# A feed-forward block with Strassen's seven products: block sums written in place, two of eight K pairs, a bank of its own for the shared product

## The chip, the cores and the metric

The kernel runs on one core of one Trainium2 chip. The time is device microseconds from start to end of one execution; it is measured several times and the median is given. Five engines work in parallel, each on its own queue of instructions in a fixed order: TensorE (PE, with its weight loads shown apart as PEld), VectorE (DVE), ScalarE (ACT), GpSimd (POOL) and SyncE (SP), which issues the transfers from memory. They wait for one another by semaphores.

## The reference

Two layers on 256 tokens of width 2048: layer 0 is a Mamba-2 mixer, layer 1 differential attention; each is followed by a SwiGLU feed-forward block of width 5632, with RMS norms around every part. Everything is float32. The change touches the two feed-forward blocks alone:

```python
def swiglu(h, w_gate, w_up, w_down):
    return (jax.nn.silu(h @ w_gate) * (h @ w_up)) @ w_down

for i in range(DEPTH):                      # DEPTH = 2
    x = x + rmsnorm(mixer(rmsnorm(x)))      # SSD in layer 0, attention in layer 1
    h = rmsnorm(x, norm_ffn_pre[i])
    x = x + rmsnorm(swiglu(h, ffn_w_gate[i], ffn_w_up[i], ffn_w_down[i]), norm_ffn_post[i])
```

Here h is 256 x 2048, the gate and up weights 2048 x 5632, the down weights 5632 x 2048.

## The kernel before

**Split numbers.** Every product of float32 numbers is made of three matmuls. A helper, `prep`, splits a piece of weights: ACT rounds it to `hi` (line 118), and DVE makes `lo` = raw minus `hi` (line 119). With the activations split likewise (`xT_hi`, `xT_lo`) a product is hi times hi, hi times lo and lo times hi, added up in one PSUM bank. A matmul takes 128 x 128 activations as its stationary side and 128 x 512 weights as its moving side.

**Where weights lie.** `rawp` has three buffers of 128 x 2048 float32 (1 MB), into which SP loads weights. `hlB` has four buffers for `hi` and four for `lo`. `accp` and `auxp` are four PSUM banks each: all eight that there are. `t512` tiles (eight buffers) hold results.

**The stage in question.** An `ffn` goes through the 5632 columns in chunks of 512. Chunk 10 runs through the plain routine `mv`; chunks 0 to 9 run two at a time through `pair` (line 200), once with the gate weights and once with the up weights: five couples of a gate call and an up call in a block, so twenty calls of `pair` in the kernel. A call computes four results of 128 x 512, named (t, c) for token half t and column half c, over eight K pairs (`kp` 0 to 7). A K pair is 256 rows of weights by 1024 columns, one `raw` buffer, loaded by two transfers of 512 KB (line 230).

- A plain K pair does the 2 x 2 by 2 x 2 block product as eight products, which is 24 matmuls, six for each (t, c). It needs one `prep`.
- A K pair of the first `NSTR` = 3 does it with Strassen's seven products (Winograd's form): 21 matmuls. For these DVE adds up four sums of weight blocks into a second tile, `sums`, which takes another of the three `rawp` buffers (lines 245 to 247); `prep` is run on three blocks of the raw weights and on the four sums, so two of the `hlB` buffers are used. Sums of activations (`form`) are made once in a block by `make_forms`. Products p1, p5 and p6 are added up in banks of `auxp`; the product that two results share is added up in the bank of (1, 1), from which DVE reads it after the third K pair, while later products still have to be added there. Then DVE makes the combinations s1, w and u (lines 262 to 265).

After the last K pair `done` adds the combination to each (t, c): for the gate into a fresh tile `g`, with Silu by ACT (lines 748, 749), for the up call into `y`, followed by the product with `g` (lines 758, 759). After an up call each `g` is turned by four transposes on PE and split again (`act_piece`, line 276), and after two, four and four chunks `out_proj` multiplies with the down weights through `mv`.

**What sets the order.** The program is written in straight lines; a scheduler gives each engine a fixed order of its own at build time and takes pool buffers as they come free. An engine whose next instruction has to wait does not go on to another.

Of the kernel before, what the change touches and what calls it, by code (L numbers as in the profile page):

```python
# [10 lines left out]
F32 = mybir.dt.float32  # L11
# [20 lines left out]
NSTR = 3  # L32
# [3 lines left out]
def trunk_kernel(ctx, tc, x_rows, x_cols, vec_cols, vec64, post_rows, lam_rows,  # L36
# [163 lines left out]
    def pair(blocks, ns, form, done):  # L200

        flush()
        acc = {}
        begun = set()

        def bank(k):
            if k not in acc:
                acc[k] = (auxp if k in ("p1", "p5", "p6") else accp).tile(
                    [P, 512], F32, tag="aux" if k in ("p1", "p5", "p6") else "acc", name=f"c{k}"
                    if isinstance(k, str) else "acc")
            return acc[k]

        def mm(k, st, hi, lo, last):
            ps = bank(k)

            again = k == (1, 1) and ns > 0
            for q, (a, b) in enumerate(((st[0], hi), (st[0], lo), (st[1], hi))):
                nc.tensor.matmul(ps, a, b, start=k not in begun, stop=last and q == 2, skip_group_check=again)  # L223
                begun.add(k)

        ss = {}
        for kp, src in enumerate(blocks):
            raw = rawp.tile([P, 4, 512], F32, tag="raw", name="raw")
            for c in range(2):
                nc.sync.dma_start(raw[:, 2 * c:2 * c + 2], src[c])  # L230
            if kp >= ns:
                hi, lo = prep(raw)
                for t in range(NT):
                    for c, slots in ((0, (2, 3)), (1, (0, 1))):
                        for j in range(2):
# [12 lines left out]
            hi, lo = prep(raw[:, 1:4])
            sh, sl = prep(sm)
            k0, k1 = 2 * kp, 2 * kp + 1  # L250
            mm("p1", x_stat(k0, 0), hi[:, 1], lo[:, 1], last)
            mm((0, 0), x_stat(k1, 0), hi[:, 2], lo[:, 2], last and ns == len(blocks))
            mm("p5", form(kp, 0), sh[:, 1], sl[:, 1], last)
            tick()
            mm((0, 1), form(kp, 3), hi[:, 0], lo[:, 0], last and ns == len(blocks))
            mm("p6", form(kp, 2), sh[:, 2], sl[:, 2], last)
            mm((1, 0), x_stat(k1, 1), sh[:, 3], sl[:, 3], last and ns == len(blocks))
            mm((1, 1), form(kp, 1), sh[:, 0], sl[:, 0], last)
            tick()
            if last:  # L260
                s1, w, u = (t512(n) for n in ("s1", "sw", "su"))
                nc.scalar.copy(s1, acc["p1"])
# [3 lines left out]
                ss.update({(0, 0): (s1, ALU.add), (0, 1): (w, ALU.add), (1, 0): (u, ALU.subtract), (1, 1): (w, ALU.add)})  # L266
# [440 lines left out]
    def ffn(wg, wu, wd, step, final):  # L707
# [36 lines left out]
        def g_done(p):  # L744
            def done(t, c, ps, ss):
                g = gt[(t, 2 * p + 1 - c)] = t512("g")
                s, op = ss[(t, c)]
                nc.vector.tensor_tensor(g, ps, s, op=op)
                nc.scalar.activation(g, g, AF.Silu, scale=rs(t))
            return done  # L750

        def u_done(p):
            def done(t, c, ps, ss):
                ch = 2 * p + 1 - c
                g = gt[(t, ch)]
                s, op = ss[(t, c)]
# [217 lines left out]
```

## Time and profile before

| | us |
|---|---|
| median of 3 runs | 2629.34 (2629.06 to 2629.64) |
| the profiled execution's own time | 2630.26 |
| its span, first to last instruction | 2628.5 |
| PE busy | 2566.6 (98%), 12210 matmuls |
| weight loads busy | 2099.3 (80%) |
| DVE busy | 1873.6 (71%) |
| ACT busy | 1308.1 (50%) |

A busy PE in this table is not PE at its peak: a matmul of 512 columns is shown with some 390 ns, while in a full pipeline one starts every 227 ns. So a matmul that starts late is seen in the spacing of the starts, that is, in how long a stretch with a known number of matmuls takes, and less in PE's idle time. The rows that follow later give such stretches.

### The profile page before, as it was taken

To read this page: it belongs to the slowest core of one execution; us is meant where nothing else is said; L and a number is where in the kernel's file an instruction comes from. 1 tells how busy PE (TensorE), PEld (TensorE's weight loads), DVE (VectorE), ACT (ScalarE), POOL (GpSimd) and SP (SyncE) were. 2 spreads that over 40 slices of the span, in tenths; PEclk is the share of its full clock that TensorE was granted. 3 is DMA by queue.
4 is the path that set the end of the run, shared out by engine and by line. 5 is a ranking of instruction groups with operands and counts; after the bars stand their busy time and mean duration, and the time that the engine had idled before them with its cause. 6 is when DMAs were issued, how large, how long until landed. Compare 5 with 4: busy or idle time off the path is not lost.

```text
span 2628.5 us, 31177 instructions
## 1 busy us (share of the span) xinstructions
PE 2566.6 (98%) x12210; PEld 2099.3 (80%) x12210; DVE 1873.6 (71%) x2250; ACT 1308.1 (50%) x1526; POOL 158.5 (6%) x164
## 2 busy tenths in 40 slices
PE   8999999999999999999999999999999999999998
PEld 7878888887877877788788788887787777887776
DVE  7888758886787577757775666556686588667864
ACT  4555555555565345435453544445654445434542
POOL 2021000120100000000001100001100000000001
PEclk9999999999999999999999999999999999999999
DMA  6545555454746445554665544544546455645463
GB/s 220 192 145 193 190 194 178 175 177 163 276 165 234 166 160 209 208 176 163 214 232 206 193 147 161 176 156 143 214 177 208 162 190 186 216 163 205 169 249 138
DMA packets 111699, 492.10 MB, mean 187 GB/s; under 512 B 10880, under 2 KB 27584, under 8 KB 75712
## 3 DMA queue, kind: packets, MB, share of 16 engines
q1 hardware_dynamic: 110896, 489.27, 53.2%
q8 instruction: 96, 1.57, 0.2%
q10 hardware_dynamic: 656, 0.85, 0.1%
q14 instruction: 51, 0.42, 0.0%
HBM read 483.71 MB, written 6.36 MB: 186 GB/s over the span
## 4 chain that ended last, share of the span: by engine, by line
PE 69%; DVE 14%; DMA 8%; ACT 4%; issue 4%; POOL 0%; SPq 0%; DVEq 0%; ACTq 0%; POOLq 0%
PE acc L167 37%; PE acc L223 11%; PE acc L192 11%; DVE lo L119 7%; PE acc L194 6%; DMA raw<-in_w_u_dram 4%; ACT hi L118 4%; DMA raw<-in_w_g_dram 4%; DVE sums L245 1%; PE sc L850 1%; DVE sums L247 1%; PE py L503 1%; DVE sums L246 1%; DVE v L428 1%; SPq L230 0%
## 5 line engine op out<-in xcount | busy, mean ns | idle before, releaser
L119 DVE TENSOR_TENSOR lo<-raw,hi 128x2048 fp32r<-128x2048 f32 (+2 forms) x488 | 931.7, 1912 | 528.6 <-ACT hi L118 528.0
L118 ACT CAST hi<-raw 128x2048 fp32r<-128x2048 f32 (+2 forms) x488 | 768.3, 1576 | 770.6 <-PE acc L167 239.3
L223 PE MATMUL acc<-hi,xT 128*128 128x512 f32 x1840 | 598.2, 394 | 5.4 <-ACT hi L118 5.1
L192 PE MATMUL acc<-xT,hi 128*128 128x512 f32 x1280 | 456.7, 400 | 0.0
L223 PEld LDWEIGHTS acc<-hi,xT 128*128 128x128 f32 x1840 | 349.4, 190 | 83.7 <-ACT hi L118 9.0
L223 PE MATMUL acc<-lo,xT 128*128 128x512 f32 x920 | 363.6, 395 | 18.9 <-DVE lo L119 18.9
L194 PE MATMUL acc<-xT,lo 128*128 128x256 f32 x1280 | 360.1, 283 | 5.8 <-DVE lo L119 5.8
L167 PE MATMUL acc<-hi,xT 128*128 128x512 f32 x1024 | 336.1, 400 | 2.3 <-ACT xT L584 2.0
L192 PEld LDWEIGHTS acc<-xT,hi 128*128 128x128 f32 x1280 | 241.7, 189 | 57.0 <-issue 1.0
L167 PE MATMUL acc<-hi,ah_f 128*128 128x512 f32 x704 | 275.2, 391 | 0.0
L167 PE MATMUL acc<-lo,ah_f 128*128 128x512 f32 x704 | 274.8, 390 | 0.0
L167 PE MATMUL acc<-hi,al_f 128*128 128x512 f32 x704 | 274.0, 389 | 0.0
L194 PEld LDWEIGHTS acc<-xT,lo 128*128 128x128 f32 x1280 | 243.5, 190 | 8.3 <-DVE lo L119 6.7
L167 PEld LDWEIGHTS acc<-hi,xT 128*128 128x128 f32 x1024 | 192.6, 189 | 48.5 <-issue 5.1
L223 PEld LDWEIGHTS acc<-lo,xT 128*128 128x128 f32 x920 | 174.6, 190 | 60.7 <-DVE lo L119 25.0
L167 PE MATMUL acc<-lo,xT 128*128 128x512 f32 x512 | 207.4, 405 | 1.6 <-DVE lo L119 1.6
L118 ACT CAST hi<-sums 128x2048 fp32r<-128x2048 f32 x60 | 114.6, 1910 | 139.0 <-DVE sums L247 85.5
L119 DVE TENSOR_TENSOR lo<-sums,hi 128x2048 fp32r<-128x2048 f32 x60 | 137.3, 2288 | 25.7 <-ACT hi L118 25.1
L167 PEld LDWEIGHTS acc<-hi,al_f 128*128 128x128 f32 x704 | 132.2, 188 | 27.4
L167 PEld LDWEIGHTS acc<-hi,ah_f 128*128 128x128 f32 x704 | 132.2, 188 | 27.0
L167 PEld LDWEIGHTS acc<-lo,ah_f 128*128 128x128 f32 x704 | 132.2, 188 | 26.8
L605 POOL TENSOR_TENSOR m<-m,wpost 128x512 f32<-128x512 f32 x24 | 44.3, 1846 | 1491.3 <-ACT junk L287 1451.6
(235 smaller groups left out, 3093.6 us busy)
## 6 DMA issues: line engine op xcount, KB each, us to landing
raw<-in_w_d_dram SPq DMA_DIRECT2D x88, 1024.0 KB, 4.8
raw<-in_w_zxbc_dram SPq DMA_DIRECT2D x80, 1024.0 KB, 4.8
raw<-in_w_g_dram SPq DMA_DIRECT2D x160, 512.0 KB, 4.4
raw<-in_w_u_dram SPq DMA_DIRECT2D x160, 512.0 KB, 5.0
raw<-in_w_qkv_dram SPq DMA_DIRECT2D x48, 1024.0 KB, 4.8
raw<-in_w_so_dram SPq DMA_DIRECT2D x32, 1024.0 KB, 4.8
raw<-in_w_ao_dram SPq DMA_DIRECT2D x16, 1024.0 KB, 4.7
mt<-acum_d SPq DMA_DIRECT2D x16, 512.0 KB, 6.7
```

The lines of the kernel that those rows point to most:

```text
L118: nc.scalar.copy(hi, raw)
L119: nc.vector.tensor_tensor(lo, raw, hi.bitcast(F32), op=ALU.subtract)
L167: nc.tensor.matmul(acc[t], a, b[:, j], start=(i == 0 and j == 0 and q == 0), stop=(i == last and j == 1 and q == 2))
L192: nc.tensor.matmul(acc[ct], hi[:, j, cs], x.rearrange("p a s -> p (a s)"), start=(i == 0 and j == 0), stop=False)
L194: nc.tensor.matmul(acc[ct][:, :S], lo[:, j, cs], x[:, 0], start=False, stop=(i == last and j == 1))
L223: nc.tensor.matmul(ps, a, b, start=k not in begun, stop=last and q == 2, skip_group_check=again)
L245: nc.vector.tensor_tensor(sm[:, 0:2], raw[:, 1:3], raw[:, 0:1].to_broadcast([P, 2, 512]), op=ALU.add)
L246: nc.vector.tensor_tensor(sm[:, 2], sm[:, 1], raw[:, 1], op=ALU.add)
L247: nc.vector.tensor_tensor(sm[:, 3], sm[:, 2], raw[:, 3], op=ALU.add)
L428: nc.vector.scalar_tensor_tensor(v, u[:, k:k + S], cwh[:, ch, k:k + 1], v, op0=ALU.mult, op1=ALU.add)
L503: nc.tensor.matmul(py[e * 64:(e + 1) * 64, a], xd[c][:, 2 * a + e], mts[c][:, 2 * a + e], start=True, stop=True)
L605: (nc.vector if n == 3 else nc.gpsimd).tensor_tensor(dst, mt, pw(n), op=ALU.mult)
```

## The change

`NSTR = 3` (K pairs 0, 1, 2) becomes `SEVEN = (3, 5)`: two K pairs with seven products, with a plain one between them, and 0, 1, 2, 4, 6, 7 plain. The sums are no longer written into a second buffer but over the raw weights, by four additions of 512 columns, after `prep` has read the raw blocks. The products that use raw blocks come first (p1, (0, 0), (0, 1)), then those that use sums. The shared product gets a bank of its own (p7), and the combinations are four tiles (s1, u, w, x), into which `done` adds the accumulators, in place of fresh `g` and `y` tiles. `make_forms` is called for n = 1 and 2 in place of 0 and 1.

```diff
-NSTR = 3
+SEVEN = (3, 5)
@@ pair
-            if kp >= ns:
+            if kp not in seven:
                 hi, lo = prep(raw)
...
-            last = kp == ns - 1
-
-            sm = rawp.tile([P, 4, 512], F32, tag="raw", name="sums")
-            nc.vector.tensor_tensor(sm[:, 0:2], raw[:, 1:3], raw[:, 0:1].to_broadcast([P, 2, 512]), op=ALU.add)
-            nc.vector.tensor_tensor(sm[:, 2], sm[:, 1], raw[:, 1], op=ALU.add)
-            nc.vector.tensor_tensor(sm[:, 3], sm[:, 2], raw[:, 3], op=ALU.add)
+            last = kp == seven[-1]
             hi, lo = prep(raw[:, 1:4])
-            sh, sl = prep(sm)
+
+            nc.vector.tensor_tensor(raw[:, 2], raw[:, 2], raw[:, 0], op=ALU.add)
+            nc.vector.tensor_tensor(raw[:, 0], raw[:, 0], raw[:, 1], op=ALU.add)
+            nc.vector.tensor_tensor(raw[:, 1], raw[:, 1], raw[:, 2], op=ALU.add)
+            nc.vector.tensor_tensor(raw[:, 3], raw[:, 3], raw[:, 1], op=ALU.add)
+            sh, sl = prep(raw)
             mm("p1", x_stat(k0, 0), hi[:, 1], lo[:, 1], last)
-            mm((0, 0), x_stat(k1, 0), hi[:, 2], lo[:, 2], last and ns == len(blocks))
-            mm("p5", form(kp, 0), sh[:, 1], sl[:, 1], last)
+            mm((0, 0), x_stat(k1, 0), hi[:, 2], lo[:, 2], False)
+            mm((0, 1), form(kp, 3), hi[:, 0], lo[:, 0], False)
             tick()
-            mm((0, 1), form(kp, 3), hi[:, 0], lo[:, 0], last and ns == len(blocks))
-            mm("p6", form(kp, 2), sh[:, 2], sl[:, 2], last)
-            mm((1, 0), x_stat(k1, 1), sh[:, 3], sl[:, 3], last and ns == len(blocks))
-            mm((1, 1), form(kp, 1), sh[:, 0], sl[:, 0], last)
+            mm("p6", form(kp, 2), sh[:, 1], sl[:, 1], last)
+            mm("p5", form(kp, 0), sh[:, 2], sl[:, 2], last)
+            mm("p7", form(kp, 1), sh[:, 0], sl[:, 0], last)
+            mm((1, 0), x_stat(k1, 1), sh[:, 3], sl[:, 3], False)
             tick()
             if last:
-                s1, w, u = (t512(n) for n in ("s1", "sw", "su"))
+                s1, u, w, x = (t512(n) for n in ("s1", "su", "sw", "sx"))
                 nc.scalar.copy(s1, acc["p1"])
                 nc.vector.tensor_tensor(u, acc["p6"], s1, op=ALU.subtract)
                 nc.vector.tensor_tensor(w, acc["p5"], u, op=ALU.add)
-                nc.vector.tensor_tensor(u, acc[(1, 1)], u, op=ALU.add)
+                nc.vector.tensor_tensor(u, acc["p7"], u, op=ALU.add)
+                nc.vector.tensor_tensor(x, acc["p7"], w, op=ALU.add)
@@ g_done, u_done
-                g = gt[(t, 2 * p + 1 - c)] = t512("g")
-                s, op = ss[(t, c)]
-                nc.vector.tensor_tensor(g, ps, s, op=op)
+                g, op = ss[(t, c)]
+                gt[(t, 2 * p + 1 - c)] = g
+                nc.vector.tensor_tensor(g, ps, g, op=op)
...
-                y = t512("y")
-                nc.vector.tensor_tensor(y, ps, s, op=op)
+                y, op = ss[(t, c)]
+                nc.vector.tensor_tensor(y, ps, y, op=op)
```

How it stands on the engines. On DVE, around the start of the first up call of a block, before: `lo` of the raw blocks, `lo` of the sums, and the sums themselves of three K pairs in a row, with the gate call's `g` in between.

```order
L245 TENSOR_TENSOR sums_7358<-raw_7355 128x1024
L119 TENSOR_TENSOR lo232_7363<-raw_7355,hi232_7362 128x1536
L246 TENSOR_TENSOR sums_7358<-sums_7358,raw_7355 128x512
L247 TENSOR_TENSOR sums_7358<-sums_7358,raw_7355 128x512
L245 TENSOR_TENSOR sums_7401<-raw_7398 128x1024
L119 TENSOR_TENSOR lo233_7367<-sums_7358,hi233_7366 128x2048
L246 TENSOR_TENSOR sums_7401<-sums_7401,raw_7398 128x512
L247 TENSOR_TENSOR sums_7401<-sums_7401,raw_7398 128x512
L748 TENSOR_TENSOR g_7325<-acc_7085,s1_7181 128x512
L119 TENSOR_TENSOR lo234_7406<-raw_7398,hi234_7405 128x1536
```

The same call on DVE now, from K pair 3 to the start of K pair 5 (after lo237 the four additions and the `lo` of the sums follow as for K pair 3):

```order
L120 TENSOR_TENSOR lo234_7450<-raw_7446,hi234_7449 128x1536
L239 TENSOR_TENSOR raw_7446<-raw_7446 128x512
L240 TENSOR_TENSOR raw_7446<-raw_7446 128x512
L241 TENSOR_TENSOR raw_7446<-raw_7446 128x512
L242 TENSOR_TENSOR raw_7446<-raw_7446 128x512
L120 TENSOR_TENSOR lo235_7458<-raw_7446,hi235_7457 128x2048
L120 TENSOR_TENSOR lo236_7490<-raw_7486,hi236_7489 128x2048
L120 TENSOR_TENSOR lo237_7521<-raw_7517,hi237_7520 128x1536
```

The tile `sums` is gone, `lo` of the raw blocks stands ahead of the additions, and a plain `lo` (236) stands between the two K pairs. The second place is the hand-over from an up call to the next gate call. On DVE before, `y` and `g` (lines 758, 759) of the up call stand among the next call's sums:

```order
L758 TENSOR_TENSOR y_8612<-acc_8372,s1_8468 128x512
L119 TENSOR_TENSOR lo279_8729<-raw_8721,hi279_8728 128x1536
L759 SCALAR_TENSOR_TENSOR g_8323<-y_8612,rs_pre0_0_6681,g_8323 128x512
L758 TENSOR_TENSOR y_8621<-acc_8380,sw_8469 128x512
L758 TENSOR_TENSOR y_8630<-acc_8388,su_8470 128x512
L759 SCALAR_TENSOR_TENSOR g_8332<-y_8621,rs_pre0_0_6681,g_8332 128x512
L759 SCALAR_TENSOR_TENSOR g_8341<-y_8630,rs_pre0_1_6816,g_8341 128x512
L758 TENSOR_TENSOR y_8639<-acc_8392,sw_8469 128x512
L119 TENSOR_TENSOR lo280_8733<-sums_8724,hi280_8732 128x2048
L759 SCALAR_TENSOR_TENSOR g_8350<-y_8639,rs_pre0_1_6816,g_8350 128x512
```

The same on DVE now (s1, sw, su and sx are the tiles that take the place of `y` and `g`):

```order
L120 TENSOR_TENSOR lo273_8640<-raw_8636,hi273_8639 128x2048
L120 TENSOR_TENSOR lo274_8693<-raw_8689,hi274_8692 128x2048
L752 TENSOR_TENSOR s1_8539<-acc_8342,s1_8539 128x512
L752 TENSOR_TENSOR sw_8541<-acc_8349,sw_8541 128x512
L753 SCALAR_TENSOR_TENSOR s1_8256<-s1_8539,rs_pre0_0_6681,s1_8256 128x512
L753 SCALAR_TENSOR_TENSOR sw_8258<-sw_8541,rs_pre0_0_6681,sw_8258 128x512
L752 TENSOR_TENSOR su_8540<-acc_8356,su_8540 128x512
L120 TENSOR_TENSOR lo275_8724<-raw_8720,hi275_8723 128x2048
L753 SCALAR_TENSOR_TENSOR su_8257<-su_8540,rs_pre0_1_6816,su_8257 128x512
L752 TENSOR_TENSOR sx_8542<-acc_8363,sx_8542 128x512
L265 TENSOR_TENSOR al_f1_3_0_8624<-pt_f1_3_0_8618,ah_f1_3_0_8623 128x512
L753 SCALAR_TENSOR_TENSOR sx_8259<-sx_8542,rs_pre0_1_6816,sx_8259 128x512
```

Two `lo` of the next call (273, 274) now stand ahead of all of these, and the `lo` of its third K pair (275) in their midst. On PE, the first eight transposes of the four `g` follow directly on the up call now; the last eight stand so, `acc_8650` and `acc_8675` being the next gate call's banks of (0, 1) and (1, 0):

```order
L219 MATMUL acc_8650<-hi273_8639,xT0_99 128x512
L271 MATMUL pt_f1_3_1_8657<-ident_86,su_8257 128x128 x4
L219 MATMUL acc_8675<-hi273_8639,xT0_99 128x512
L219 MATMUL acc_8675<-lo273_8640,xT0_99 128x512
L219 MATMUL acc_8675<-hi273_8639,xT0_99 128x512 x2
L271 MATMUL pt_f1_2_1_8666<-ident_86,sx_8259 128x128 x4
```

Before, the last eight stood behind 23 matmuls of the next call; now four of them stand behind its first 12 and four behind its first 16. Where the down products follow on an up call, four stand behind their first 10 and four behind their first 14 to 16. Outside of the calls of `pair` and the hand-overs next to them the order on each engine is the same as before.

## Rows read from the trace of the kernel before

**Rows 1.** The page: engines' busy time, share of the span, instructions.
```profile
PE   2566.6 (98%) x12210; PEld 2099.3 (80%) x12210; DVE 1873.6 (71%) x2250; ACT 1308.1 (50%) x1526; POOL 158.5 (6%) x164
```

**Rows 2.** Windows, line 223 alone: first 87 matmuls (K pairs 0 to 3), 20 calls.
```profile
core 0: us, PE busy (x) PEld busy (x), PEclk, DMA share, GB/s
774.81:795.34 20.53, 20.25 (x88) 16.11 (x88) 1.00 0.65 228
817.12:841.13 24.01, 22.14 (x88) 17.32 (x87) 0.93 0.62 208
...
sum 449.04, PE 417.60 PEld 328.74; mean PE 20.88 PEld 16.44
```

**Rows 3.** The same view: last 96 matmuls (K pairs 4 to 7), 20 calls.
```profile
795.34:817.12 21.78, 21.78 (x98) 18.02 (x96) 1.00 0.52 176
...
2416.60:2439.04 22.44, 21.93 (x97) 17.83 (x95) 1.00 0.50 176
...
sum 436.01, PE 435.50 PEld 358.55; mean PE 21.77 PEld 17.93
```

**Rows 4.** Windows, line 167 alone: two stretches of down products behind an up call.
```profile
862.90:930.07 67.17, 65.96 (x288) 53.85 (x288) 1.00 0.43 152
1108.87:1197.79 88.92, 87.71 (x384) 71.85 (x384) 1.00 0.47 163
```

**Rows 5.** Timeline of SP, 823 to 836: start, duration, what.
```profile
823.54 0.80 SPq L230 DMA_DIRECT2D raw<-in_w_u_dram  x2
...
825.21 0.80 SPq L230 DMA_DIRECT2D raw<-in_w_u_dram  x2
...
827.41 0.97 SPq L230 DMA_DIRECT2D raw<-in_w_u_dram  x2
...
834.14 0.80 SPq L230 DMA_DIRECT2D raw<-in_w_u_dram  x2
```

**Rows 6.** Timeline of ACT in the second call: start, duration, what, idle before.
```profile
822.12 1.92 ACT L118 CAST hi<-sums 128x2048 fp32r<-128x2048 f32 x1
829.87 1.91 ACT L118 CAST hi<-raw 128x2048 fp32r<-128x2048 f32 x1 [5.83 <-DMA raw<-in_w_u_dram]
...
832.53 1.90 ACT L118 CAST hi<-raw 128x2048 fp32r<-128x2048 f32 x1 [0.27 <-DMA raw<-in_w_u_dram]
836.06 1.90 ACT L118 CAST hi<-raw 128x2048 fp32r<-128x2048 f32 x1 [1.63 <-DMA raw<-in_w_u_dram]
839.88 1.91 ACT L118 CAST hi<-raw 128x2048 fp32r<-128x2048 f32 x1 [1.92 <-DMA raw<-in_w_u_dram]
```

**Rows 7.** Timeline of DVE in the second call.
```profile
825.10 2.28 DVE L119 TENSOR_TENSOR lo<-sums,hi 128x2048 fp32r<-128x2048 f32 x1
831.82 2.29 DVE L119 TENSOR_TENSOR lo<-raw,hi 128x2048 fp32r<-128x2048 f32 x1 [4.43 <-ACT hi L118]
```

**Rows 8.** Groups by form, 774 to 863: count | busy us, mean ns | idle before.
```profile
L119 DVE TENSOR_TENSOR lo<-raw,hi 128x1536 fp32r<-128x1536 f32 x5 | 8.8, 1752 | 1.4 <-ACT hi L118 1.4
L118 ACT CAST hi<-raw 128x1536 fp32r<-128x1536 f32 x4 | 5.9, 1484 | 2.8 <-PE acc L223 1.5 <-DMA raw<-in_w_u_dram 1.2 <-PE cp L223 0.2
L247 DVE TENSOR_TENSOR sums<-sums,raw 128x512 f32<-128x512 f32 x4 | 2.8, 690 | 0.1
```

**Rows 9.** Timeline of DVE at the end of the second call.
```profile
859.01 0.69 DVE L758 TENSOR_TENSOR y<-acc,s 128x512 f32<-128x512 f32 x1 [2.56 <-PE acc L223]
859.62 2.28 DVE L119 TENSOR_TENSOR lo<-raw,hi 128x2048 fp32r<-128x2048 f32 x1
861.82 0.75 DVE L759 SCALAR_TENSOR_TENSOR g<-y,rs_pre,g 128x512 f32<-128x512 f32 x1
862.48 0.68 DVE L758 TENSOR_TENSOR y<-acc,sw 128x512 f32<-128x512 f32 x1
```

**Rows 10.** The page, groups: PE's matmuls of line 223, idle time last.
```profile
L223 PE MATMUL acc<-hi,xT 128*128 128x512 f32 x1840 | 598.2, 394 | 5.4 <-ACT hi L118 5.1
L223 PE MATMUL acc<-lo,xT 128*128 128x512 f32 x920 | 363.6, 395 | 18.9 <-DVE lo L119 18.9
```

**Rows 11.** DMA issues: KB each, median us to landing.
```profile
x<-xr_d SPq DMA_DIRECT2D x8, 512.0 KB, 7.8
```

More of the change, by code (lines that the diff above doesn't have):

```diff
@@ L198, in ws, with pair @@
             tick()
-    def pair(blocks, ns, form, done):
+    def pair(blocks, seven, form, done):
         flush()
         acc = {}
[L209 to L216, printed above, removed]
+        end = len(blocks) - 1
         def mm(k, st, hi, lo, last):
-            ps = bank(k)
-            again = k == (1, 1) and ns > 0
+            first = k not in acc
+            if first:
+                acc[k] = (auxp.tile([P, 512], F32, tag="aux", name="cp") if isinstance(k, str) else
+                          accp.tile([P, 512], F32, tag="acc", name="acc"))
             for q, (a, b) in enumerate(((st[0], hi), (st[0], lo), (st[1], hi))):
-                nc.tensor.matmul(ps, a, b, start=k not in begun, stop=last and q == 2, skip_group_check=again)
-                begun.add(k)
+                nc.tensor.matmul(acc[k], a, b, start=first and q == 0, stop=last and q == 2)
         ss = {}
@@ L230, in pair @@
                 nc.sync.dma_start(raw[:, 2 * c:2 * c + 2], src[c])
-            if kp >= ns:
+            if kp not in seven:
                 hi, lo = prep(raw)
                 for t in range(NT):
-                    for c, slots in ((0, (2, 3)), (1, (0, 1))):
+                    for c, e in ((0, 2), (1, 0)):
                         for j in range(2):
-                            e = slots[j]
-                            mm((t, c), x_stat(2 * kp + j, t), hi[:, e], lo[:, e], kp == len(blocks) - 1 and j == 1)
-                        if kp == len(blocks) - 1:
+                            mm((t, c), x_stat(2 * kp + j, t), hi[:, e + j], lo[:, e + j], kp == end and j == 1)
+                        if kp == end:
                             done(t, c, acc[(t, c)], ss)
@@ L264, in pair @@
                 nc.vector.tensor_tensor(w, acc["p5"], u, op=ALU.add)
-                nc.vector.tensor_tensor(u, acc[(1, 1)], u, op=ALU.add)
-                ss.update({(0, 0): (s1, ALU.add), (0, 1): (w, ALU.add), (1, 0): (u, ALU.subtract), (1, 1): (w, ALU.add)})
+                nc.vector.tensor_tensor(u, acc["p7"], u, op=ALU.add)
+                nc.vector.tensor_tensor(x, acc["p7"], w, op=ALU.add)
+                ss.update({(0, 0): (s1, ALU.add), (0, 1): (w, ALU.add), (1, 0): (u, ALU.subtract), (1, 1): (x, ALU.add)})
     def split(dst_hi, dst_lo, src):
@@ L755, in done @@
                 g = gt[(t, ch)]
-                s, op = ss[(t, c)]
-                y = t512("y")
-                nc.vector.tensor_tensor(y, ps, s, op=op)
+                y, op = ss[(t, c)]
+                nc.vector.tensor_tensor(y, ps, y, op=op)
                 nc.vector.scalar_tensor_tensor(g, y, rs(t), g, op0=ALU.mult, op1=ALU.mult)
@@ L773, in ffn @@
                 nc.sync.dma_start(xr_d[t][h].rearrange("p (e k) -> p e k", e=2), xr_of[(t, h)])
-        later(1, lambda: make_forms(0))
-        later(4, lambda: make_forms(1))
+        for k, n in enumerate(sorted({kp // 2 for kp in SEVEN})):
+            later(1 + 3 * k, lambda n=n: make_forms(n))
         mv([wu[10, k] for k in range(4)], u_stat, u_evac, LAG2)
@@ L780, in ffn @@
                 if c < 10 and c % 2 == 0:
-                    pair(twos(wg, c), NSTR, form, g_done(c // 2))
-                    pair(twos(wu, c), NSTR, form, u_done(c // 2))
+                    pair(twos(wg, c), SEVEN, form, g_done(c // 2))
+                    pair(twos(wu, c), SEVEN, form, u_done(c // 2))
             last = pi == len(parts) - 1
```

## The prediction

> **What bounds the kernel now.** I read the page first: PE is shown busy for 98% of the span, DVE for 71%, ACT for 50% [rows 1]. That looks like a kernel in which nothing is left to gain on PE, and the change gives PE more to do. So I next asked how long PE takes for a known number of matmuls in the stage that the change touches. A call of `pair` has 3 x 21 + 5 x 24 = 183 matmuls on line 223. The last 96 of each call (K pairs 4 to 7) take 21.78 us, and 436.01 us over all twenty calls: 436.01 / 1920 = 0.227 us for a matmul, with one call alone longer, by 0.66 us [rows 3]. That is the full pipeline. The first 87 of each call (three K pairs with seven products and one plain) would take 19.75 us at that pace, and take 20.5 to 24 us, 449.04 us over twenty calls [rows 2]. Of these, 56 transposes fall in the windows, at 0.11 us each (the 67.17 us of the first stretch of down products less 288 x 0.227, over the 16 transposes in it [rows 4]): 6.2 us. What is lost to waits is 449.04 - 1740 x 0.227 - 6.2 = 47.8 us, and with the 0.66 us some 48.5 us. In a window with a long wait the granted clock is 0.93 instead of 1.00 [rows 2], a part of it spent at the lower of the clock's two levels; what that costs is in the 48.5.
>
> Then I asked what those waits are. In the second call ACT sits idle for 5.83 us until K pair 3's weights land, and DVE for 4.43 us until ACT is done [rows 6, 7]. Neither engine is short of time there; the load came late. SP issued the three loads behind the K pairs with sums at 823.54, 825.21 and 827.41, each when a `lo` was done [rows 5, 7], and ACT could start on them at 829.87, 832.53 and 836.06, 6.3, 7.3 and 8.65 us after issue; a load that has the queues to itself, issued at 834.14, takes 5.7 us to 839.88 [rows 5, 6]. So what bounds PE is three weight buffers: three K pairs in a row take two each, six tiles go through three buffers, and loads are issued late and in a bunch.
>
> A rule bears on the first reading. The groups of line 223 show PE idle for 5.4 + 18.9 us only [rows 10], about half of what the spacing gives. The Trainium skill (Perfetto Trace Analysis, Identifying the Most-Contended Engine) says that busy time of matmuls misjudges the headroom, because they are pipelined, and that the share of weight loads shows it. By the idle time the change could save 24.3 us at most and would end near 2629.3 - 24.3 + 13.6 = 2618.6 us. The trace sides with the rule: weight loads are busy 73% of the first 87 matmuls' windows and 82% of the last 96's [rows 2, 3].
>
> **The change, part by part.** All of it is taken against the profiled execution (span 2628.5 us, its own time 2630.26 us); the median of the runs is 0.9 us under that, and the differences are applied to the median.
>
> *One seven-product K pair less in a call.* 42 + 144 = 186 matmuls instead of 183: 60 more in the kernel, 60 x 0.227 = **+13.6 us**, all on the path, since PE is what the stage runs at.
>
> *Waits of the first 87 matmuls.* Each K pair now holds one weight buffer. Whether PE then waits I work out along one call, from its start at 0, at 24 x 0.227 = 5.45 us for a plain K pair and 4.77 for one with seven products: K pair 3 starts at 16.35, 4 at 21.1, 5 at 26.6, 6 at 31.35, 7 at 36.8, and the end is at 42.25. The four `hi` and `lo` buffers come free in order. The tight one is K pair 5. Its raw part needs the buffer of K pair 2, free at some 16.5; then `hi` 1.48, `lo` 1.75, four additions at 0.69, `hi` of the sums 1.92, `lo` of the sums 2.28 [rows 6 to 8], one behind the other because the sums are written over what is read: 10.2 us, ready at 26.8. PE asks for it after nine matmuls of K pair 5, at 28.65. So 1.85 us to spare. K pair 3 may start some 14 us earlier against its own due time of 18.4 and has over 5 us to spare; K pair 6's `lo` ends at 29.0 against 31.35. Nothing waits: **-48.5 us**, of which the bounds are dealt with below. DVE has less to do as well: for each seven-product K pair 6.8 us, and a plain one takes 2.29.
>
> *Hand-over from call to call.* The buffer of K pair 5 is held until 26.8, those of 6 and 7 until 29.0 and 31.2, so the next call's first three loads go out 2.2 us apart. No row shows just that; the nearest is the bunch above (6.3, 7.3, 8.65 us), the other end is 5.7 us for each. I take 6, 6.8 and 7.5, nearer to the bunch. With `hi` and `lo` behind them the next call's first two blocks are ready at 37.0 and 40.0, well before 42.25. But DVE's order now puts both ahead of the up call's `y` and `g` (the order on DVE at the hand-over, above), so these begin at 3.2 us into K pair 7 instead of on the accumulator. At the spacing of 0.6 to 0.66 us that such rows have, and 2.2 for the `lo` among them [rows 9], the four `g` are done at 5.1, 5.75, 9.2 and 11.05. PE ends its call at 5.45, does eight transposes (0.9), 12 matmuls to 9.1, waits 0.2 for the third, does four and four matmuls to 10.6, and waits 0.5: 0.7 us at each of four such places. At the six places where down products follow, the same count gives 0 to 0.3 us. Gate to up has no transposes, and the banks are emptied in time: the one of (0, 0) at 3.9 against 5.45. With a little more, below, I book **+5 us** for all ten; at the slow end, with loads at 8.65 us, DVE comes 1 us later and each place costs up to 1.8, 18 us in all.
>
> *Edits with one answer.* The p7 bank frees (1, 1) of DVE's reading; the fourth combination costs DVE 0.69 us in K pair 7, when it has time. `g` and `y` are written over the combinations: same instructions, fewer tiles. `make_forms` has the same work at the same place. But its tiles hold the buffers into which x is fetched again for the last down product, now until K pair 5 of the last up call instead of K pair 2, and SP issues these transfers (7.8 us to landing [rows 11]) among the first loads of down weights; one such load 3 us later costs some 0.5 us, twice in the kernel, within the 5 us.
>
> Sum: -48.5 + 13.6 + 5 = -29.9 us, 2629.3 - 29.9 = 2599.4: **2600 us**. The bounds: 2594 with no wait left, 2612 with the slow hand-over.
>
> **Rivals.**
>
> *The price sticks to each seven-product K pair.* 48.5 / 60 = 0.81 us each; forty remain, 32.3 us, and the time is 2629.3 - 16.2 + 13.6 = 2626.7 us, within 0.2%, about what a measurement here can tell from no change. For it: 6.8 us of DVE work stand against 4.77 us of PE. Against it: DVE idles for 4.43 us in the midst of the wait [rows 7], and a plain K pair with 3.1 us of DVE's time to spare now stands before, between and behind. 7%.
>
> *Sums over their sources come too late (slower).* The chain of K pair 5 can't begin its sums before both splits of the raw part are done, and this load's buffer is held meanwhile. Each microsecond past the 1.85 to spare costs 20 us over the calls; it eats up the whole gain at 1.85 + 34.9 / 20 = 3.6 us late, and at 4.5 late the time is 2594.4 + 20 x 2.65 = 2647 us. For it: the chain is serial, and loads in a bunch have been 3 us late [rows 5, 6]. Against it: this load is issued over 10 us before it is needed. 5%.
>
> *Hand-overs eat more.* The next call's first product now goes straight into the bank of (0, 0), and transposes wait for a DVE that has put two `lo` first. If DVE comes 2 us later than I count, it is some 2 us more at each of the ten places: 2620 us. The Trainium skill (Perfetto Trace Analysis, Matmuls) has a rule that speaks for this one: independent groups should rotate through banks, so that emptying one overlaps the next group's matmuls; the four accumulator banks here are taken again at once, where before p1 went first to a spare one. The rows let the bank be empty 1.5 us ahead of need, so the rule costs nothing by them; no run so far shows it. 8%.
>
> **How the numbers follow.** The forecast has 80%. It and the third rival are faster by over 0.2% (88%), the first is within it (7%), the second slower (5%). The range goes from 2592 (the lower bound, less 2 us for stretches at the lower clock that I may have undercounted) to 2618, into the third rival.
>
> **What would show it.** Right: 186 matmuls of line 219 in a call, some 42.3 us for a call without transposes; no ACT idle of over 3 us behind a load in front of a K pair of `pair` that PE then waits for; a granted clock of 1.00 in all twenty calls; idle of PE's transposes behind `g` in place of the waits for `lo`, some 0.5 us at each hand-over. Wrong: PE waiting for `lo` of the sums of K pair 5 (second rival), at K pair 3 and at 5 alike (first), or a `y` that begins later than 4 us into K pair 7 (third).

## The result

The changed kernel takes **2600.32 us** (median of 4, 2598.74 to 2601.97) beside 2629.49 us (2629.06 to 2629.74) for the kernel before: a ratio of 0.9889, 95% interval 0.9872 to 0.9906. 2600 us was forecast. In a later comparison it took 2600.49 us and the kernel before 2622.68: 22 us less there, a ratio of 0.9914. The kernel before differs by some us from one comparison to another, so that experiments of different comparisons are set side by side by their ratios.

The page of the changed kernel, busy time by engine, as [rows 1]:

```profile
PE 2561.4 (99%) x12270; PEld 2105.6 (81%) x12270; DVE 1815.8 (70%) x2230; ACT 1276.9 (49%) x1506; POOL 158.4 (6%) x164
```

PE is busy for 5 us less with 60 more matmuls, and the span is 30.2 us shorter (2628.5 to 2598.3). As with [rows 1], such a line tells hardly anything. The windows of the calls tell it, line 219 alone (the matmuls of `pair`, line 223 before), one row for each call of 186 matmuls. Columns as in [rows 2].

```profile
816.59:858.75 42.16, 42.16 (x187) 34.73 (x185) 1.00 0.56 202
926.25:968.40 42.15, 42.15 (x186) 34.92 (x186) 1.00 0.52 188
...
1011.36:1055.11 43.75, 42.82 (x186) 34.86 (x187) 1.00 0.52 187
1055.11:1097.75 42.64, 42.32 (x187) 34.74 (x185) 1.00 0.55 191
...
sum 852.00, PE 846.87 PEld 696.09; mean PE 42.34 PEld 34.80
```

Eleven of the twenty calls take 42.15 to 42.17 us: 42.16 / 186 = 0.2267 us for each matmul, through K pairs with seven products and plain ones alike, with no wait of PE in them. Six more hold four or eight transposes (42.66 us, and 43.51 to 43.96). Three up calls, such as the one at 1055.11, take 42.46 to 42.64: the first transpose behind them waits 0.3 to 0.5 us for `s`. The granted clock is 1.00 in all twenty. The sum was 449.04 + 436.01 = 885.05 us [rows 2, 3]; it is 33.05 us less. Everything outside of the calls is 2.85 us more, of which 1.8 us are 16 transposes that now stand ahead of a call instead of in it (0.11 us each). The groups of the page agree; the idle time in the last column was 5.4 and 18.9 us [rows 10]:

```profile
L219 PE MATMUL acc<-hi,xT 128*128 128x512 f32 x2080 | 656.8, 390 | 0.0
...
L219 PE MATMUL acc<-lo,xT 128*128 128x512 f32 x1040 | 405.0, 389 | 0.0
```

The K pair with least time to spare is 5. Timeline of DVE in the call that starts at 816.59:

```profile
834.66 1.76 DVE L120 TENSOR_TENSOR lo<-raw,hi 128x1536 fp32r<-128x1536 f32 x1 [2.71 <-ACT hi L119]
836.45 0.69 DVE L239 TENSOR_TENSOR raw<-raw 128x512 f32<-128x512 f32 x1
...
838.63 0.69 DVE L242 TENSOR_TENSOR raw<-raw 128x512 f32<-128x512 f32 x1
841.38 6.70 DVE L120 TENSOR_TENSOR lo<-raw,hi 128x2048 fp32r<-128x2048 f32 x3 [2.06 <-ACT hi L119]
```

The last row holds three `lo`; the first, of the sums, is done 2.29 us on, at 843.67, that is 27.1 us after the call's start; PE asks for it at 28.65. So 1.6 us are to spare, where 1.85 were worked out. The row also shows something that matters further on: DVE stands still for 2.06 us in the midst of the chain, until ACT has rounded the sums, and nothing else on its queue may pass.

### The profile page after: what moved, and what is told of

Its sections match the earlier page's. It is cut to its first block, busy times and chain, and to the rows that moved or that the text cites. A ratio compares the mean times of both kernels' runs of the same rounds, so it can differ in the third digit from the quotient of the medians.

```text
span 2598.3 us, 31297 instructions
## 1 busy us (share of the span) xinstructions
PE 2561.4 (99%) x12270; PEld 2105.6 (81%) x12270; DVE 1815.8 (70%) x2230; ACT 1276.9 (49%) x1506; POOL 158.4 (6%) x164
## 4 chain that ended last, share of the span: by engine, by line
PE 86%; DVE 6%; issue 3%; ACT 2%; DMA 2%; POOL 0%; DVEq 0%; SPq 0%; ACTq 0%; POOLq 0%
PE acc L168 39%; PE acc L219 23%; PE acc L193 11%; PE acc L195 6%; PE cp L219 3%; DVE lo L120 2%; ACT hi L119 2%; PE sc L844 1%; DMA raw<-in_w_d_dram 1%; DMA raw<-in_w_g_dram 1%; PE py L498 1%; DVE v L423 1%; PE pt_f L271 1%; PE ptx L574 0%; PE pyt L508 0%
## 5 line engine op out<-in xcount | busy, mean ns | idle before, releaser
L120 DVE TENSOR_TENSOR lo<-raw,hi 128x2048 fp32r<-128x2048 f32 (+2 forms) x528 | 1030.4, 1961 | 609.2 <-ACT hi L119 608.8
L119 ACT CAST hi<-raw 128x2048 fp32r<-128x2048 f32 (+2 forms) x528 | 851.1, 1618 | 924.8 <-PE acc L168 250.4
L219 PE MATMUL acc<-hi,xT 128*128 128x512 f32 x2080 | 656.8, 390 | 0.0
L219 PEld LDWEIGHTS acc<-hi,xT 128*128 128x128 f32 x2080 | 390.5, 188 | 80.5
L219 PE MATMUL acc<-lo,xT 128*128 128x512 f32 x1040 | 405.0, 389 | 0.0
L168 PE MATMUL acc<-hi,xT 128*128 128x512 f32 x1024 | 334.9, 399 | 2.3 <-ACT xT L579 2.0
L168 PEld LDWEIGHTS acc<-hi,xT 128*128 128x128 f32 x1024 | 191.8, 188 | 48.1 <-issue 5.1
L219 PEld LDWEIGHTS acc<-lo,xT 128*128 128x128 f32 x1040 | 195.3, 188 | 40.2
L168 PE MATMUL acc<-lo,xT 128*128 128x512 f32 x512 | 206.7, 404 | 1.6 <-DVE lo L120 1.6
L124 DVE SCALAR_TENSOR_TENSOR lo<-raw,cols,hi 128x512 fp32r<-128x512 f32 x128 | 92.7, 771 | 52.0 <-ACT hi L123 51.7
L168 PEld LDWEIGHTS acc<-lo,xT 128*128 128x128 f32 x512 | 96.4, 188 | 23.7 <-issue 3.9
```

What stands on the lines that cost most here:

```text
L119: nc.scalar.copy(hi, raw)
L120: nc.vector.tensor_tensor(lo, raw, hi.bitcast(F32), op=ALU.subtract)
L124: nc.vector.scalar_tensor_tensor(lo[:, j], raw[:, j], scale[j], hi[:, j].bitcast(F32), op0=ALU.mult, op1=ALU.subtract)
L168: nc.tensor.matmul(acc[t], a, b[:, j], start=(i == 0 and j == 0 and q == 0), stop=(i == last and j == 1 and q == 2))
L219: nc.tensor.matmul(acc[k], a, b, start=first and q == 0, stop=last and q == 2)
```

## The experiments

In each, "waits" are read from the spacing of the starts of matmuls or from the table of what PE waited for.

### Two seven-product K pairs, first in a row, and nothing else

The kernel before with two in place of three:

```diff
-NSTR = 3
+NSTR = 2
```

> The kernel before with NSTR = 2: K pairs 0 and 1 with seven products, everything else as it was (sums in a buffer of their own, shared bank). 186 matmuls a call, as in the change. Theory (bunched loads: six tiles through three weight buffers hold the load of K pair 3 back until 6.4 us into the call): with four tiles the load of K pair 3 goes out some 2 us before the call starts and lands by 4.2 us, well before 9.5, so the 48.5 us of waits go and the kernel comes to 2629.5 - 48.5 + 13.6 + 2 to 5 = 2597 to 2600 us, without spacing, without sums in place. Rival (a price of 0.81 us on each seven-product K pair, DVE's 6.8 us against PE's 4.77): 40 x 0.81 stays, about 2627 us. Rival (spacing and sums in place are what removes the waits): one wait of 1 to 2 us a call stays, 2615 to 2635 us.

Measured: 2597.78 us (2 runs), ratio 0.9893 [0.9859, 0.9927]. The windows of its twenty calls, line 223 alone, sum up to

```profile
sum 851.64, PE 847.34 PEld 695.49; mean PE 42.37 PEld 34.77
```

which is the changed kernel's 852.00. So the whole gain comes from the third K pair that became plain. Spacing, sums in place and a bank for p7 together add nothing to it that can be measured, and two K pairs in a row with two weight buffers each go through three buffers with hardly a wait.

### The sums in place, three in a row

The kernel before with the additions and the order of `prep` of the changed one, K pairs 0, 1, 2:

```diff
-            sm = rawp.tile([P, 4, 512], F32, tag="raw", name="sums")
...
             hi, lo = prep(raw[:, 1:4])
-            sh, sl = prep(sm)
+            nc.vector.tensor_tensor(raw[:, 2], raw[:, 2], raw[:, 0], op=ALU.add)
...
+            sh, sl = prep(raw)
```

> The kernel before with one part of the change: sums written over the raw weights, after both splits; still K pairs 0, 1, 2, shared bank, products in the old order. 183 matmuls a call. Theory (loads): six tiles become three, the load wait goes; but the chain of a K pair is now serial, 10.2 us, and in a row the third one starts when the first one's hi buffer is free (2.7 us into the call), so its sums come at 13.2 us against 10.9 needed: a wait of about 2.3 us takes the place of the old one, 2629.5 - 48.5 + 46 = about 2627 us (2610 to 2640), and the waiting rows are lo of the sums, no longer loads. Rival (buffers alone are the cause, spacing is idle): 2629.5 - 48.5 = 2581 us.

Measured: 2691.65 us (2 runs), ratio 1.0251 [1.0216, 1.0285]: 64 us slower, where no change (2627) was expected. The table of what PE waited for (us in total, times, longest) is led by

```profile
PE cp L223 <- ACT hi L118: 56.1, 28, 3.1
```

the `hi` of sums. One part of the change, alone, costs twice what the whole change gains.

### The changed kernel with three in a row

```diff
-SEVEN = (3, 5)
+SEVEN = (0, 1, 2)
```

> The changed kernel with SEVEN = (0, 1, 2): sums in place, p7 bank, raw products first, but three in a row. 183 matmuls a call. Theory (serial chain without spacing): the third K pair's sums come at about 13.2 us against 9.54 + 9 x 0.227 = 11.6 needed, 1.6 us of wait in each call: 2600.3 - 13.6 + 32 = 2619 us (2605 to 2630). Rival (sums in place alone do it): 2600.3 - 13.6 = 2587 us. Rival (0.81 us for each seven-product K pair): 2629 us or so.

Measured: 2694.64 us (2 runs, 2688.27 and 2701.00), ratio 1.0262 [1.0195, 1.0329], much as in the last experiment; 2619 was expected. Timeline of DVE in its second call, K pairs 1 and 2:

```profile
826.86 3.96 DVE L120 TENSOR_TENSOR lo<-raw,hi 128x2048 fp32r<-128x2048 f32 x2 [2.05 <-ACT hi L119]
830.85 0.69 DVE L239 TENSOR_TENSOR raw<-raw 128x512 f32<-128x512 f32 x1
...
833.03 0.69 DVE L242 TENSOR_TENSOR raw<-raw 128x512 f32<-128x512 f32 x1
835.74 4.50 DVE L120 TENSOR_TENSOR lo<-raw,hi 128x2048 fp32r<-128x2048 f32 x2 [2.02 <-ACT hi L119]
```

From one chain's `lo` of the sums to the next's, 826.86 to 835.74, it is 8.88 us: 3.99 for `lo` of the sums and `lo` of the next raw blocks, 2.87 for four additions, 2.02 of standing still. PE is through such a K pair in 4.77. I had let three chains overlap, and on DVE's fixed order they can't. So sums in place need plain K pairs between; this is what the spacing is for, and together they come out even with `NSTR = 2`.

### The changed kernel with sums in a tile of their own

```diff
+            sm = rawp.tile([P, 4, 512], F32, tag="raw", name="sums")
+            nc.vector.tensor_tensor(sm[:, 2], raw[:, 2], raw[:, 0], op=ALU.add)
+            nc.vector.tensor_tensor(sm[:, 0], raw[:, 0], raw[:, 1], op=ALU.add)
+            nc.vector.tensor_tensor(sm[:, 1], raw[:, 1], sm[:, 2], op=ALU.add)
+            nc.vector.tensor_tensor(sm[:, 3], raw[:, 3], sm[:, 1], op=ALU.add)
             hi, lo = prep(raw[:, 1:4])
-            nc.vector.tensor_tensor(raw[:, 2], raw[:, 2], raw[:, 0], op=ALU.add)
...
-            sh, sl = prep(raw)
+            sh, sl = prep(sm)
```

> The changed kernel with one part undone: sums in a weight buffer of their own again, K pairs 3 and 5, p7 bank and order of products kept. 186 matmuls a call. Theory (loads): with plain K pairs before, between and behind, no load is bunched so far that PE waits: 2600 us, within 4. Rival (sums in place are what frees the loads): part of the waits comes back, 2608 us or more, with ACT idle behind loads at K pairs 4 to 6.

Measured: 2598.27 us (2 runs), ratio 0.9895 [0.9861, 0.9929]. With two K pairs, spaced, it makes no difference that can be measured where the sums are written.

### Three seven-product K pairs, spaced

Now the number of the kernel before, K pairs 1, 3 and 5; `make_forms` takes K pairs 1 and 3, then 5. First with the sums in place:

```diff
-SEVEN = (3, 5)
+SEVEN = (1, 3, 5)
+GROUPS = ((1, 3), (5,))
```

> The changed kernel with a third seven-product K pair, spaced: SEVEN = (1, 3, 5), sums in place; the forms of K pairs 1 and 3 lie in one buffer, those of 5 in another. 183 matmuls a call, as before the change. Theory (waits come from seven-product K pairs in a row, not from their number): 60 matmuls fewer, 2600.3 - 13.6 = 2587 us; DVE then has some 80 us of work in a couple of calls against 84 of PE, so up to 0.5 us a call may come on top, 2587 to 2597 us. Rival (each seven-product K pair costs PE 0.81 us, whatever stands between): 2600.3 - 13.6 + 48.5 = 2635 us.

Measured: 2607.14 us (4 runs), ratio 0.9941 [0.9925, 0.9958]: 10 us over the range expected, and far from the rival's 2635. Then the same with the sums in a tile of their own (the edit shown above):

> The run with SEVEN = (1, 3, 5), but the sums in a weight buffer of their own: six tiles in eight K pairs go through three buffers, as before the change, with plain K pairs between. 183 matmuls a call. Theory (loads held back because the six tiles come in a row): no long wait for loads, within 5 us of the run with sums in place, 2583 to 2597 us. Rival (six tiles a call are too many for three buffers): waits of 2 us a call come back, about 2627 us.

Measured: **2590.12 us** (4 runs, 2590.03 to 2593.40), ratio 0.9877 [0.9857, 0.9896], 17 us below its twin, where 5 at most were expected. Six tiles a call go through three buffers, as in the kernel before, and there is no bunch of late loads: in the second call they go out at 823.95, 827.16, 833.37 and 837.49. What differs from the kernel before is where the three K pairs stand, and besides it the bank for p7, the order of products and the tiles of the combinations; no run has the first without the others. Timelines of DVE in the second call; first, sums in place:

```profile
822.01 6.16 DVE L121 TENSOR_TENSOR lo<-raw,hi 128x2048 fp32r<-128x2048 f32 x3 [2.06 <-ACT hi L120]
...
833.13 6.16 DVE L121 TENSOR_TENSOR lo<-raw,hi 128x2048 fp32r<-128x2048 f32 x3 [2.05 <-ACT hi L120]
```

and in a tile of their own:

```profile
828.85 2.29 DVE L121 TENSOR_TENSOR lo<-sums,hi 128x2048 fp32r<-128x2048 f32 x1 [2.06 <-ACT hi L120]
...
839.48 2.29 DVE L121 TENSOR_TENSOR lo<-sums,hi 128x2048 fp32r<-128x2048 f32 x1 [2.06 <-ACT hi L120]
```

From chain to chain, one seven-product and one plain K pair, DVE takes 11.12 us in place and 10.63 with a tile of its own, since additions on DVE (833.26 to 835.1) and the rounding of the raw blocks on ACT (832.77 to 834.25) then run side by side. PE takes 4.77 + 5.45 = 10.22. Both periods are longer, so DVE falls behind by 0.9 or 0.4 us a chain. What PE waits for the larger one stands in its table as

```profile
PE acc L220 <- ACT hi L120: 13.1, 16, 1.1
```

It does not wait in every call. Windows of line 220 (the matmuls of `pair` in these kernels): two gate calls with sums in place, the first behind down products, the second behind an up call, and that second call with sums in a tile of their own:

```profile
927.28:968.76 41.48, 41.48 (x184) 34.35 (x183) 1.00 0.55 203
1011.62:1058.10 46.48, 43.13 (x183) 33.88 (x184) 1.00 0.48 174
```

```profile
1010.57:1053.66 43.09, 42.46 (x183) 34.14 (x184) 1.00 0.53 190
```

The first takes 183 x 0.2267 = 41.48 us, the pace without a wait. DVE falls behind there as well, but from a lead; its `lo` of the sums of K pairs 1, 3 and 5 begin at

```profile
927.55 4.66 DVE L121 TENSOR_TENSOR lo<-raw,hi 128x2048 fp32r<-128x2048 f32 x2 [2.05 <-ACT hi L120]
...
941.19 6.16 DVE L121 TENSOR_TENSOR lo<-raw,hi 128x2048 fp32r<-128x2048 f32 x3 [2.05 <-ACT hi L120]
...
952.31 4.50 DVE L121 TENSOR_TENSOR lo<-raw,hi 128x2048 fp32r<-128x2048 f32 x2 [2.05 <-ACT hi L120]
```

and are done 2.29 us on, that is 4.9, 1.5 and 0.6 us before PE is at the products with sums. Of the 16.4 us by which all twenty calls differ (858.79 and 842.37), 12.1 stand in the four gate calls behind an up call, where DVE has the four results to finish first, and 3.7 in the up calls behind those.

### The first addition on GpSimd

To the kernel with three spaced K pairs and sums in place:

```diff
-            nc.vector.tensor_tensor(raw[:, 2], raw[:, 2], raw[:, 0], op=ALU.add)
+            nc.gpsimd.tensor_tensor(raw[:, 2], raw[:, 2], raw[:, 0], op=ALU.add)
```

> The run with SEVEN = (1, 3, 5) and sums in place, with the first of the four additions moved from DVE to GpSimd. DVE has 0.7 us less to do in each of 60 K pairs. Theory (DVE's order is what is left in the three-spaced kernel): equal or up to 5 us faster than it. Rival (the chain of a K pair gets longer, since a GpSimd addition of 128x512 takes some 1.8 us in other rows against 0.7, and PE waits for it): 60 x 1.1 = up to 66 us slower.

Measured: 2635.42 us (4 runs), ratio 1.0054 [1.0034, 1.0074], 28 us above its twin. DVE is relieved of 60 additions, and the chain becomes longer. The group of POOL, and two chains on DVE:

```profile
L240 POOL TENSOR_TENSOR raw<-raw 128x512 f32<-128x512 f32 x60 | 77.4, 1290 | 1147.7 <-DVE lo L121 753.6 <-DMA raw<-in_w_g_dram 337.9 <-DMA raw<-in_w_u_dram 56.2
```

```profile
822.92 6.39 DVE L121 TENSOR_TENSOR lo<-raw,hi 128x2048 fp32r<-128x2048 f32 x3 [1.46 <-ACT hi L120]
830.76 0.69 DVE L241 TENSOR_TENSOR raw<-raw 128x512 f32<-128x512 f32 x1 [1.45 <-POOL raw L240]
...
834.95 6.17 DVE L121 TENSOR_TENSOR lo<-raw,hi 128x2048 fp32r<-128x2048 f32 x3 [2.05 <-ACT hi L120]
...
846.72 4.49 DVE L121 TENSOR_TENSOR lo<-raw,hi 128x2048 fp32r<-128x2048 f32 x2 [2.05 <-ACT hi L120]
```

The addition takes 1.29 us instead of 0.69, all of it in the chain (DVE idles for 1.45 until it is done), and the period is 12.03 us and then 11.77 instead of 11.12. What counts here is the period of the chain, and not how much work DVE has.

### Four, spaced, with sums of their own

To the fastest kernel above:

```diff
-SEVEN = (1, 3, 5)
-GROUPS = ((1, 3), (5,))
+SEVEN = (0, 2, 4, 6)
+GROUPS = ((0, 2), (4, 6))
```

> Seven products in K pairs 0, 2, 4 and 6, sums in a weight buffer of their own: 180 matmuls a call, 60 fewer than with three such K pairs, 13.6 us less if PE waits for nothing. My theory (what counts is the period of DVE's queue for one seven-product and one plain K pair, idle time for the hi of the sums included): with sums of their own that period was 10.63 us (828.85 to 839.48, with three spaced K pairs), PE's is 4.77 + 5.45 = 10.22, so with no spare plain K pair left in a call DVE falls behind by 4 x 0.41 = 1.6 us a call, 33 us over twenty, and the gain turns: some 2609 us beside 2590 for three. Rival (busy time of DVE counts: 2 x 2.29 + 1.75 + 4 x 0.60 = 8.7 us in 10.22, so it keeps up): some 2577 us.

Measured: 2647.17 us (4 runs), ratio 1.0090 [1.0075, 1.0106]. The theory that DVE's busy time counts (2577) is refuted. Mine had the direction, and neither the size (2609) nor the place, as the windows show. Gate calls that follow on a down product take 40.80 us, 180 matmuls without a wait: a lag of 0.4 us a chain does not reach PE inside such a call. What is slow are the gate calls behind an up call and the up calls behind those (line 220 alone; the last two rows are one couple):

```profile
926.68:967.48 40.80, 40.80 (x181) 33.80 (x180) 1.00 0.55 199
...
1010.21:1061.03 50.82, 44.55 (x181) 34.32 (x182) 0.97 0.46 166
1061.03:1109.03 48.00, 44.09 (x181) 33.98 (x179) 0.96 0.57 203
```

and the start of one of them, all engines (PE, PEld, DVE, ACT, POOL, then the granted clock):

```profile
1010.90:1016.30 5.40, 1.95 (x14) 1.42 (x13) 5.40 (x8) 1.93 (x4) 0.00 (x0) 1.00 0.00 0
1016.30:1018.30 2.00, 1.42 (x4) 1.17 (x5) 2.00 (x4) 0.78 (x1) 0.00 (x0) 0.74 0.00 0
1018.30:1020.30 2.00, 2.00 (x5) 1.13 (x5) 1.18 (x2) 2.00 (x2) 0.00 (x0) 0.50 0.78 270
```

and what PE waits for in it:

```profile
1016.88 0.50 PE L220 MATMUL cp<-lo,xT 128*128 128x512 f32 x1 [2.75 <-DVE lo L121]
```

DVE is busy all through: the combinations of K pair 6, the four `y` and `g`, and the sums of the next call's K pair 0 come together. PE waits 2.75 us for a `lo`, and its granted clock is lower behind that. I had counted the lag over a call and not this pile-up at its end.

### Three from K pair 0

```diff
-SEVEN = (1, 3, 5)
-GROUPS = ((1, 3), (5,))
+SEVEN = (0, 2, 4)
+GROUPS = ((0, 2), (4,))
```

> Three spaced K pairs with sums of their own, as in the fastest kernel so far, but K pairs 0, 2 and 4 instead of 1, 3 and 5, so that two plain ones end a call. My theory: same 183 matmuls a call, no waits inside a call, and DVE is freer at the hand-over: 2586 to 2590 us. Rival: the first K pair of a call is then the one whose sums, combinations and outputs of the call before meet on DVE, and PE waits there: over 2595 us.

Measured: 2611.76 us (5 runs), ratio 0.9955 [0.9942, 0.9969]; my theory said 2586 to 2590, the rival over 2595, and the rival is right. Same work, same number of matmuls, 20 us above the kernel with K pairs 1, 3 and 5 that ran beside it (2591.79, in the next experiment; its transposes stand later, which changes nothing there). The longest row of the products of `pair` in PE's table is

```profile
PE acc L220 <- DVE sw L751: 6.5, 4, 1.7
```

and DVE's timeline at the start of the second call, 816.93, why:

```profile
814.46 2.29 DVE L121 TENSOR_TENSOR lo<-sums,hi 128x2048 fp32r<-128x2048 f32 x1 [2.06 <-ACT hi L120]
816.67 0.68 DVE L751 TENSOR_TENSOR s<-acc,s 128x512 f32<-128x512 f32 x1
817.27 2.28 DVE L121 TENSOR_TENSOR lo<-raw,hi 128x2048 fp32r<-128x2048 f32 x1
819.47 0.68 DVE L751 TENSOR_TENSOR sw<-acc,sw 128x512 f32<-128x512 f32 x1
```

The next call's chain stands on DVE ahead of the last call's results, and the bank that `sw` empties is wanted earlier than 819.5. This row is 6.5 us of the 20; in the same table transposes wait 5.8 us for `s` and `sw`, and products 3.2 for a `hi` or `lo`.

### Transposes of g later

In the changed kernel, and in the fastest one beside it in another comparison:

```diff
-                later(2, piece)
+                later(4, piece)
```

> The changed kernel with the transposes of the four g of a couple put off by two more steps, so that 12 or more matmuls stand ahead of them and as many more ahead of the last ones. Theory (the 5.5 us that PE waits at the ten hand-overs is transposes standing too near to the g that DVE makes late): these waits go, 2600.3 - 5.5 = 2595 us. Rival (what waits there is only moved, to the next load or accumulator bank): 2600 us, unchanged.

Measured: 2598.70 us (4 runs), ratio 0.9911 [0.9894, 0.9927], as without the edit (0.9889 and 0.9914); the 2595 of my theory did not come, and the rival is right. PE waits less ahead of those transposes, 1.0 us instead of 2.6, and waits for a bank instead:

```profile
PE acc L219 <- DVE sx L752: 3.1, 3, 1.5
```

> The fastest kernel so far (K pairs 1, 3, 5, sums of their own) with the transposes of g two ticks later. My theory: like the same edit on the changed kernel, it moves the waits of the transposes to the accumulators of the next call's first products and changes nothing: 2588 to 2592. Rival: the waits at the hand-overs are of their own and go: 2584.

Measured: 2591.79 us (4 runs), ratio 0.9882 [0.9866, 0.9898], as without the edit (0.9877) and as expected. So the hand-over is set by when DVE is done with the four results, and the transposes' place only chooses who waits for it.

### The changed kernel again

> The changed kernel itself, beside the other three on the same chip, so that their differences are not between chips: 2598 to 2601 us, 8 to 10 us above three spaced K pairs with sums of their own.

Measured: 2600.49 us (6 runs), ratio 0.9914 [0.9898, 0.9931]. In this comparison the kernel with three spaced K pairs and later transposes is 8.7 us below it, with 60 matmuls less (13.6 us) and some more waiting. Of the two versions with three spaced K pairs I would keep the one without that edit (2590.12 us, ratio 0.9877). Beside the changed kernel itself only the one with the edit was measured; its slowest run, 2595.06, is below the changed kernel's fastest, 2596.32.

Not tried: the kernel before with a fourth weight buffer, which would show whether it is the number of buffers that holds the loads back, or DVE's 6.8 us for a K pair in which PE takes 4.77, three times in a row: the loads of [rows 5] go out when DVE is done with a `lo`, and no run takes the two apart. There is no room for it in SBUF beside the other pools.

## Why the prediction was right, and where not

**What bounds the kernel.** Confirmed. The pace of 0.227 held (0.2267), and what the first 87 matmuls had lost could be had back, though nearly all of it by the one K pair that became plain. The smaller reading by PE's idle time, 2618.6 us, was wrong, as the rule on busy time in the Trainium skill (Perfetto Trace Analysis, Identifying the Most-Contended Engine) has it: weight loads were busy 687.29 of 885.05 us in the calls, 78%, and are busy 696.09 of 852.00, 82%, which [rows 3] showed as the share of a stretch without waits.

**The terms.** 60 more matmuls at +13.6 us: held. Waits in the first 87 matmuls, -48.5: gone, since eleven calls take 42.15 to 42.17 us and the others only transposes and waits at hand-overs more. Hand-overs, +5 us: of the calls' 852.00 us, 843.2 are matmuls (20 x 42.16) and 4.4 are 40 transposes, so 4.4 us are waits, and with some 1.1 us outside of the calls they make 5.5. At the four places from up to gate the calls take 43.75, 43.95, 43.96 and 43.51 us; without 42.16 of matmuls and eight transposes (0.9) PE waits 0.5 to 0.9 at each, where 0.7 was worked out. At two of the six places where down products follow (behind the up calls at 1055.11 and 2195.44) the call's end and the down products together take 1.4 us more than without waits or than before, where 0 to 0.3 was worked out. The sum was -29.9 us and the span fell by 30.2. In the later comparison the kernel before was 7 us faster and the change was worth 22 us; the terms were checked on the two profiled executions alone, so that their closeness to 30.2 is in part luck. DVE at the end of the call above, whose K pair 7 starts at 853.3:

```profile
856.10 0.68 DVE L752 TENSOR_TENSOR s<-acc,s 128x512 f32<-128x512 f32 x1
...
859.22 2.28 DVE L120 TENSOR_TENSOR lo<-raw,hi 128x2048 fp32r<-128x2048 f32 x1
861.42 0.74 DVE L753 SCALAR_TENSOR_TENSOR su<-su,rs_pre 128x512 f32<-128x512 f32 x1
...
863.28 0.74 DVE L753 SCALAR_TENSOR_TENSOR sx<-sx,rs_pre 128x512 f32<-128x512 f32 x1
```

`y` begins at 2.8 us, worked out 3.2; the third and the fourth `g` are done at 8.9 and 10.7, worked out 9.2 and 11.05. The order behind the two `lo` is as forecast, with a `lo` in its midst, and everything is 0.3 to 0.4 us earlier.

**The cause, half right.** "three K pairs in a row take two each, six tiles go through three buffers" named three things at once. Six tiles a call are no hindrance (three spaced K pairs with sums of their own: no row of PE's table is a wait of these products), and two K pairs in a row with two tiles each hardly one. It takes three in a row with two tiles each for PE to wait for the late and bunched loads of [rows 5 to 7]. "Each K pair now holds one weight buffer" was given as the reason why the waits go; it isn't needed, as the first experiment and the one with sums in a tile of their own show. I had not asked which part of the change carries the gain.

**The rivals.** A price for each seven-product K pair is refuted (0.81 us each, 2626.7): forty remain, and PE waits in none. Sums that come too late did not come about in this kernel (1.6 us to spare), and the mechanism is real: the same chains three in a row cost 64 us and more, and three spaced ones some 17, in calls where DVE has no lead. One chain was rightly counted; that DVE's queue makes chains exclude one another, at 8.88 us from one to the next, was in no step of it, and is why my expectations of 2627 and 2619 us for three in a row fell short by 65 and 76. Hand-overs that eat more: not here. The rule on rotating banks (the Trainium skill, Perfetto Trace Analysis, Matmuls) would have changed nothing for this kernel, in which no call waits for a bank at its start. Where DVE empties the banks later, with K pair 0 first, PE does wait for one (6.5 us), so the rule applies from the point at which the emptying is late.

## What to carry to other kernels

Cost a pipeline by the period of its chain on an engine with a fixed order, the standing still in it included, and set it against the time in which PE uses up what one period makes; busy shares of 70% hide that a chain of 11.1 us feeds a stage that wants one every 10.2. Then ask with what lead each call begins: the longer period cost nothing in gate calls behind down products and some 3 us in each of those behind an up call. A change with several parts should be costed part by part with the others left out: here the smallest one (one K pair fewer) carried all, and another one alone cost 64 us. Writing in place saves a buffer and takes away an overlap; in none of these runs did it pay.

## What was new about the hardware

- An addition on DVE of 128 x 512 float32 is shown with 0.69 us. In the sums in place, where each instruction uses or overwrites what the one before it touched, the next starts 0.73 us on (836.45 to 838.63, three steps); an unrelated one starts 0.61 us on (859.01 to 859.62 in [rows 9]).
- The same addition took 1.29 us on GpSimd, and DVE's next one waited 1.45 us behind the `lo` ahead.
- A wait of PE of 2.75 us cost more than itself. In the kernel with four K pairs PE was busy for 1.95 of 5.40 us; the granted clock was 1.00 then, 0.74 in the next 2 us and 0.50 in the 2 us behind, that is, the lower of its two levels (1.2 of 2.4 GHz), with 5 matmuls and 2.00 us busy. Matmuls start 0.43 us apart there instead of 0.227 (1017.61, 1018.04, 1018.47, 1018.89), and the thirteen from 1016.88 to 1022.09 take 5.21 us instead of 2.95. The 0.93 of a window with a long wait in [rows 2] is of this kind: two of its microseconds, behind a wait of 1.83 us, have 0.70.

```profile
834.00:836.00 2.00, 1.84 (x6) 1.47 (x7) 1.97 (x4) 0.43 (x1) 0.00 (x0) 0.70 0.41 125
```
